# A two-layer decoder trunk on one core: the masked link of the triangular inversion is made on ScalarE before the row chain, not on GpSimd within it

## The chip, the cores and the metric

The kernel runs on one core of one Trainium2 chip. The metric is device time in microseconds (us) of one execution; lower is better. The kernel before takes 1342.59 us (median of 3 runs, 1339.93 to 1345.52). All times below are us unless marked ns.

## What is computed

A decoder trunk with two layers on 256 tokens of width 1024, batch 1, all in float32. Each layer applies three sub-layers, each followed by a residual layer norm:

```
x <- LN(alpha*x + 0.5*SwiGLU_1(x))      # width 2816
x <- LN(alpha*x + Mixer(x))
x <- LN(alpha*x + 0.5*SwiGLU_2(x))
```

The mixer projects its input with one wide matrix and sums three gated branches: an RWKV-7 recurrence (8 heads of 64), a chunked gMLP and an RG-LRU recurrence. The recurrence of RWKV-7 is what matters here:

```
def step(state, inp):
    sa = einsum('bhvk,bhk->bhv', state, -kk_t)
    state = state * w_t + sa (x) (kk_t * a_t) + v_t (x) k_t
    return state, einsum('bhvk,bhk->bhv', state, r_t)
```

## The kernel before, in words

**Matrix products.** Each float32 product is made from three products of split halves: a weight block of 128 x 1024 is loaded by SyncE's DMA queue (`raw`, 3 buffers), ScalarE casts its high half (`whi`, L91), VectorE subtracts to get the low half (`wlo`, L93), and TensorE multiplies (L205 to L207). The blocks come in the fixed order of their use and are converted some blocks ahead.

**The mixer as a chain and a filler.** `Mixer.run` advances two generators. The chain (`rwkv`) is the recurrence: it is turned into chunks of 64 tokens, and for each chunk and head a unit lower-triangular 64 x 64 matrix must be inverted (`invert`), 32 of them in all, after which four rounds of `step` carry the state on. The filler (`others`) is the rest of the mixer: projections `z`, gates `g`, branch products `p` and the parts of gMLP and RG-LRU (`lx`, `lg`, `ls`, `ly`, `sp`, `ot`). Each `yield` gives an amount of time; the filler is advanced until it has covered it. Chain instructions have a higher priority. A list scheduler then fixes the order of every engine's queue from priorities and its own estimate of times, so a small edit can move instructions of other parts too. On the chip each engine runs its queue strictly in that order.

**The inversion.** It works on blocks of 16 rows. VectorE transposes the scores of each matrix into `X` (L848) and picks the diagonal blocks into `U` (L851, L852; `U` and the growing inverse `Ti` are the two halves of the tile `UT`). Then GpSimd runs the **row chain**: for each of 15 steps a product (L864, `X<-UT`) and a subtraction (L865, `UT<-UT,X`), each waiting for the one before it. VectorE spreads the result to a 32-row layout (L882, `X<-UT`) and transposes it twice (L885 into `Rd`, L886 into `Tt`). TensorE multiplies `UB` by `Tt` (L892, tile `y`), ScalarE copies it (L894, `Y`), TensorE multiplies by `Rd` (L899, `z`), VectorE subtracts (L900) and transposes (L901); a second pair of products (L910, `y`; L917, `z`) makes the 64-row inverse `R`, from which L926 and L938 make what the rounds (`up` L969, `s` L953) read.

`UB` is the **masked link**: the 16 columns 16 to 31 of each 32-column block of scores, with rows 0 to 15 of each 32 set to zero, and zeros in columns 0 to 15. Before, GpSimd makes it in four multiplications by the constant `bmask` (L879), one for each quarter of the partitions, written in the program after the row chain's loop:

```
            for u, h, rows in halves:
                c0 = ca[u] + 32 * h
                pool.tensor_tensor(UB[rows], SC[u][rows, :, c0:c0 + 32],
                                   T.bmask[rows].rearrange("p (a b) -> p a b", a=1).to_broadcast([32, 16, 32]), ALU.mult)
```

The scheduler places them within the row chain on GpSimd's queue.

Of the kernel before, what the change touches and what calls it, by code (L numbers as in the profile page):

```python
# [9 lines left out]
AF = mybir.ActivationFunctionType  # L10
ALU = mybir.AluOpType
PSUM = bass.MemoryType.PSUM
P = 128
# [102 lines left out]
class Trunk:  # L116
# [33 lines left out]
    def mixer_constants(self):  # L150
        nc, const = self.nc, self.const

        def t(name, shape):
            return const.tile(shape, F32, name=name)

        pool = nc.gpsimd
        self.identr = const.tile([P, P], F32R, name="identr")
        nc.vector.tensor_copy(self.identr, self.ident)

        self.ones64 = t("ones64", [P, P])  # L160
        self.mean64 = t("mean64", [P, P])
        for tl, v in ((self.ones64, 1.0), (self.mean64, 1.0 / 64)):
            pool.memset(tl, 0.0)
            for h in range(2):
                pool.memset(tl[64 * h:64 * h + 64, 64 * h:64 * h + 64], v)


        rar = t("smask", [P, 3, 64])
        pool.memset(rar, 1.0)
        for rows in (slice(0, 64), slice(64, P)):  # L170
            pool.affine_select(out=rar[rows], in_=rar[rows], compare_op=ALU.is_ge, fill=0.0, base=0,
                               pattern=[[0, 3], [1, 64]], channel_multiplier=-1)
            pool.affine_select(out=rar[rows, 1, :], in_=rar[rows, 1, :], compare_op=ALU.is_ge, fill=0.0, base=-1,
                               pattern=[[1, 64]], channel_multiplier=-1)
        self.smask = [rar[:, u:u + 2].rearrange("p a b -> p (a b)") for u in range(2)]

        self.restart = t("restart", [P, 8, C])
        pool.memset(self.restart, 1.0)
        pool.memset(self.restart[:, :, 0:1], 0.0)

        self.bsel = t("bsel", [P, 2])
        pool.memset(self.bsel, 0.0)
        for h in range(4):

            pool.affine_select(out=self.bsel[32 * h:32 * h + 32, 0:1], in_=self.bsel[32 * h:32 * h + 32, 0:1],
                               compare_op=ALU.is_ge, fill=1.0, base=-16, pattern=[[0, 1]], channel_multiplier=1)
            pool.affine_select(out=self.bsel[32 * h:32 * h + 32, 1:2], in_=self.bsel[32 * h:32 * h + 32, 1:2],
                               compare_op=ALU.is_ge, fill=1.0, base=15, pattern=[[0, 1]], channel_multiplier=-1)

        self.bmask = t("bmask", [P, 32])  # L190
        pool.memset(self.bmask, 0.0)
        nc.vector.tensor_scalar(self.bmask[:, 16:32], self.bmask[:, 16:32], self.bsel[:, 0:1], None, ALU.add)

        self.hsel = t("hsel", [P, 2])
        pool.memset(self.hsel, 0.0)
        for h in range(4):
            pool.memset(self.hsel[32 * h:32 * h + 32, h % 2:h % 2 + 1], 1.0)
# [325 lines left out]
class Mixer:  # L523
# [156 lines left out]
    def rwkv(self):  # L680
        T, nc, l = self.T, self.nc, self.l
        v, act, mmul = nc.vector, nc.scalar, nc.tensor.matmul
        zwa, k, r, vv = self.zwa, self.k, self.r, self.v
        w2, a2 = self.w2a2[0:64], self.w2a2[64:P]
        sg, a, n2, ARV, BK, PC, bonus, Ps, Pis = {}, {}, {}, {}, {}, {}, {}, {}, {}
# [108 lines left out]
        SC, BKT, AT, SV, W1, W2T, O = {}, {}, {}, {}, {}, {}, {}  # L794
# [45 lines left out]
        def invert():  # L840

            pool = nc.gpsimd
            units, halves = [slice(0, 64), slice(64, P)], [(u, h, slice(64 * u + 32 * h, 64 * u + 32 * h + 32)) for u in range(2) for h in range(2)]
            ca = [64, 0]
            X = self.mt([P, 16, 32], "X")
            for u, h, rows in halves:
                c0 = ca[u] + 32 * h
# [3 lines left out]
            v.tensor_scalar_mul(U, X[:, :, 0:16], T.bsel[:, 0:1])  # L851
            v.scalar_tensor_tensor(U, X[:, :, 16:32], T.bsel[:, 1:2], U, ALU.mult, ALU.add)  # L852

            pool.memset(Ti, 0.0)
            pool.affine_select(out=Ti, in_=Ti, compare_op=ALU.not_equal, fill=1.0, base=0, pattern=[[1, 16], [-1, 16]],
                               channel_multiplier=0)
# [4 lines left out]
            for t in range(15):  # L861
# [11 lines left out]
                    act.copy(xx[q], px)  # L873
                if t % 2:
                    yield 1.4
            UB = self.mt([P, 16, 32], "UB")
            for u, h, rows in halves:
                c0 = ca[u] + 32 * h
                pool.tensor_tensor(UB[rows], SC[u][rows, :, c0:c0 + 32],  # L879
                                   T.bmask[rows].rearrange("p (a b) -> p a b", a=1).to_broadcast([32, 16, 32]), ALU.mult)  # L880
            for b in range(2):
                v.tensor_scalar_mul(E[:, :, 16 * b:16 * b + 16], Ti, T.bsel[:, b:b + 1])  # L882
            R = self.sp.tile([P, 16, 64], F32, tag="b4", name=T.n("R"), bufs=2)
# [6 lines left out]
            for n in range(16):  # L890
                for u, h, rows in halves:
                    mmul(ps[rows, n, :], UB[rows, n, :], Tt[rows, n, :], start=True, stop=True)  # L892
            Y = self.mt([P, 16, 32], "Y")
# [150 lines left out]
        yield from scaled(tune["prep"], scores(1))  # L1044
        bonus_of(1)
        yield from scaled(tune["inv"], invert())
        yield from scaled(tune["step"], both(chunks(0), chunks(1)))
        yield from scaled(tune["post"], both(post(0), post(1)))
# [375 lines left out]
```

## Time and profile before

| | value |
|---|---|
| median of 3 runs | 1342.59 us (1339.93 to 1345.52) |
| the profiled execution's own time | 1344.46 us |
| its span in the trace | 1342.7 us |
| mean granted TensorE clock | 0.986 |
| TensorE busy | 1304.1 us (97%) |
| VectorE busy | 847.1 us (63%) |
| ScalarE busy | 647.6 us (48%) |
| GpSimd busy | 96.6 us (7%) |
| mean busy share of the 16 DMA engines, HBM traffic | 56%, 170 GB/s |

The profiled execution took 1344.46 us; the 1.8 us beside its span lie outside the recorded instructions. Busy time is the time in which an engine had an instruction under way. "Granted clock" is the share of TensorE's full clock of 2.4 GHz that the chip gave it; 0.5 is its lower level, 1.2 GHz. An average over the whole span hides the two mixers, which run from about 240 to 460 us and from about 890 to 1120 us; the rows below come mostly from them.

### The profile page before, as it was taken

The page shows a single profiled execution, that of the slowest core. Times are in us where ns is not written, and L with a number is a line of the kernel's source. Part 1 is how long each engine was busy: PE and PEld are TensorE (multiplying, and loading weights), DVE is VectorE, ACT ScalarE, POOL GpSimd, SP SyncE. Part 2 cuts the span into 40 slices and gives each one's busy share as a digit, 9 for nine tenths or more (in the row PEclk, how much of TensorE's full clock was granted, in tenths as well). Part 3 has the DMA queues.
Part 4 walks back from the last instruction along what each step waited for, and adds up shares of the span by engine and source line. Part 5 has one row for each costly group of instructions (what it writes and reads, how often), then busy time and mean ns, then how long its engine had stood idle before and what let it go on. Part 6 is the DMA issues. An engine that isn't in the chain of part 4 may idle for free.

```text
span 1342.7 us, 25628 instructions
## 1 busy us (share of the span) xinstructions
PE 1304.1 (97%) x10807; PEld 1231.3 (92%) x10807; DVE 847.1 (63%) x1144; ACT 647.6 (48%) x865; POOL 96.6 (7%) x154
## 2 busy tenths in 40 slices
PE   8999999997899999999999999999969999999997
PEld 8999999996899999999899999999968998999996
DVE  5655576777576665454665555777866667664444
ACT  5545436643844545344445354375448454444441
POOL 1000000005000020000000000001050002100000
PEclk9999999989999999999999999999979999999999
DMA  7686654634236647766646776464432466477661
GB/s 242 207 255 202 207 168 133 182 95 126 65 111 193 209 147 220 220 188 186 192 138 208 243 213 203 125 186 129 126 95 65 146 200 208 140 230 218 191 188 52
DMA packets 184548, 229.98 MB, mean 171 GB/s; under 512 B 8144, under 2 KB 165840, under 8 KB 184432
## 3 DMA queue, kind: packets, MB, share of 16 engines
q1 hardware_dynamic: 183792, 226.24, 55.2%
q0 software_dynamic: 640, 2.10, 0.6%
q8 instruction: 85, 1.39, 0.4%
q14 instruction: 31, 0.25, 0.1%
HBM read 227.26 MB, written 1.05 MB: 170 GB/s over the span
## 4 chain that ended last, share of the span: by engine, by line
PE 87%; ACT 4%; DVE 3%; POOL 3%; DMA 2%; issue 1%; SPq 0%; DVEq 0%; ACTq 0%; POOLq 0%
PE w L206 11%; PE w L205 11%; PE w L207 11%; PE dn L207 6%; PE dn L206 6%; PE dn L205 6%; PE gate L206 3%; PE gate L207 3%; PE gate L205 3%; PE zr L207 2%; PE zr L206 2%; PE zr L205 2%; DMA raw<-in_ffn_w_dram 2%; PE pb L205 2%; PE pb L207 2%; PE pb L206 2%
## 5 line engine op out<-in xcount | busy, mean ns | idle before, releaser
L93 DVE TENSOR_TENSOR wlo<-raw,whi 128x1024 fp32r<-128x1024 f32 (+1 forms) x314 | 381.9, 1220 | 241.0 <-ACT whi L91 239.1
L91 ACT CAST whi<-raw 128x1024 fp32r<-128x1024 f32 (+1 forms) x322 | 331.5, 1033 | 361.3 <-DMA raw<-in_ffn_w_dram 131.8
L205 PE MATMUL w<-xT,whi 128*128 128x256 f32 x1280 | 363.1, 284 | 0.0
L206 PE MATMUL w<-xT,whi 128*128 128x256 f32 x1280 | 362.8, 283 | 0.0
L207 PE MATMUL w<-xT,wlo 128*128 128x256 f32 x1280 | 362.8, 283 | 0.0
L206 PEld LDWEIGHTS w<-xT,whi 128*128 128x128 f32 x1280 | 245.9, 192 | 1.5
L205 PEld LDWEIGHTS w<-xT,whi 128*128 128x128 f32 x1280 | 246.0, 192 | 1.2
L207 PEld LDWEIGHTS w<-xT,wlo 128*128 128x128 f32 x1280 | 246.1, 192 | 0.0
L93 DVE TENSOR_TENSOR w<-raw,w 128x1024 fp32r<-128x1024 f32 x88 | 107.7, 1224 | 124.3 <-ACT w L91 123.8
L91 ACT CAST w<-raw 128x1024 fp32r<-128x1024 f32 x88 | 92.3, 1048 | 134.5 <-DMA raw<-in_ffn_w_dram 131.8
L205 PE MATMUL dn<-w,g 128*128 128x512 f32 x352 | 137.4, 390 | 0.4 <-ACT g L210 0.4
L206 PE MATMUL dn<-w,g 128*128 128x512 f32 x352 | 137.4, 390 | 0.0
L207 PE MATMUL dn<-w,g 128*128 128x512 f32 x352 | 136.6, 391 | 0.0
L205 PE MATMUL gate<-xT,whi 128*128 128x256 f32 x384 | 111.2, 290 | 1.8 <-DVE xc L1138 1.8
L207 PE MATMUL gate<-xT,wlo 128*128 128x256 f32 x384 | 111.3, 290 | 0.0
L206 PE MATMUL gate<-xT,whi 128*128 128x256 f32 x384 | 111.1, 289 | 0.0
L207 PEld LDWEIGHTS dn<-w,g 128*128 128x128 f32 x352 | 66.1, 188 | 14.1 <-DVE g L211 0.3
L205 PEld LDWEIGHTS dn<-w,g 128*128 128x128 f32 x352 | 66.3, 188 | 13.2 <-ACT g L210 1.0
L205 PEld LDWEIGHTS gate<-xT,whi 128*128 128x128 f32 x384 | 75.0, 195 | 2.9 <-issue 2.8
L206 PEld LDWEIGHTS dn<-w,g 128*128 128x128 f32 x352 | 66.1, 188 | 12.3
L206 PEld LDWEIGHTS gate<-xT,whi 128*128 128x128 f32 x384 | 74.8, 195 | 0.9 <-issue 0.2
L207 PEld LDWEIGHTS gate<-xT,wlo 128*128 128x128 f32 x384 | 74.9, 195 | 0.7 <-issue 0.2
(335 smaller groups left out, 2281.0 us busy)
## 6 DMA issues: line engine op xcount, KB each, us to landing
raw<-in_ffn_w_dram SPq DMA_DIRECT2D x264, 512.0 KB, 4.5
raw<-in_w_in_dram SPq DMA_DIRECT2D x108, 512.0 KB, 4.2
raw<-in_p_branch_dram SPq DMA_DIRECT2D x24, 512.0 KB, 3.8
raw<-in_w_out_dram SPq DMA_DIRECT2D x16, 512.0 KB, 4.3
ln_g<-in_ln_g_dram SPq DMA_DIRECT2D x8, 256.0 KB, 5.2
ln_b<-in_ln_b_dram SPq DMA_DIRECT2D x8, 256.0 KB, 6.1
bd<-in_bd_dram SPq DMA_DIRECT2D x6, 256.0 KB, 5.4
ln_g<-in_ln_g_dram POOLq DMA_DIRECT2D x4, 256.0 KB, 4.3
```

The source lines that it names most:

```text
L91: self.last_act = self.nc.scalar.copy(hi[:, s:s + w], t[:, s:s + w]).ins
L93: eng.tensor_tensor(lo[:, s:s + w], t[:, s:s + w], hi[:, s:s + w], ALU.subtract)
L205: mm(out, a[0], b[0], start=start, stop=False)
L206: mm(out, a[0], b[1], start=False, stop=False)
L207: mm(out, a[1], b[0], start=False, stop=stop)
```

## The change

`UB` is made by ScalarE, ahead of the row chain. GpSimd sets its columns 0 to 15 to zero, and ScalarE copies columns 16 to 31 with a scale per partition (`bsel`, 1 or 0), one ACTIVATE with the function Identity for each quarter of the partitions. The four multiplications and the constant `bmask`, with its memset on GpSimd and its fill on VectorE, are gone. `UB` is allocated before `xx`, so the tiles of the mixer's pool that follow it lie in other slots.

```
@@ mixer_constants
-        self.bmask = t("bmask", [P, 32])
-        pool.memset(self.bmask, 0.0)
-        nc.vector.tensor_scalar(self.bmask[:, 16:32], self.bmask[:, 16:32], self.bsel[:, 0:1], None, ALU.add)
@@ invert
             v.scalar_tensor_tensor(U, X[:, :, 16:32], T.bsel[:, 1:2], U, ALU.mult, ALU.add)
 
+            UB = self.mt([P, 16, 32], "UB")
+            pool.memset(UB[:, :, 0:16], 0.0)
+            for u, h, rows in halves:
+                c0 = ca[u] + 32 * h
+                act.activation(UB[rows, :, 16:32], SC[u][rows, :, c0 + 16:c0 + 32], AF.Identity, scale=T.bsel[rows, 0:1])
+
             pool.memset(Ti, 0.0)
...
                 if t % 2:
                     yield 1.4
-            UB = self.mt([P, 16, 32], "UB")
-            for u, h, rows in halves:
-                c0 = ca[u] + 32 * h
-                pool.tensor_tensor(UB[rows], SC[u][rows, :, c0:c0 + 32],
-                                   T.bmask[rows].rearrange("p (a b) -> p a b", a=1).to_broadcast([32, 16, 32]), ALU.mult)
```

The change also moves instructions in the scheduler's order. Outside the stretch from the inversion to the end of each mixer's rounds the queues hold the same instructions in the same order, save for the dropped constant. Line numbers after the edits differ by 3 or 4 (L882 is L879 after, L899 is L896).

VectorE's queue in the first mixer, at the end of the row chain, before (`X<-UT` is the first instruction behind the row chain, `wlo` a low half of a weight, `xc` a step of the RG-LRU convolution, `ogT` gMLP's output):

```order
L93 TENSOR_TENSOR wlo_3676<-raw_3582,whi_3675 128x1024
L1138 SCALAR_TENSOR_TENSOR xc_3574<-lx_3575,vecs_1159,xc_3574 128x255
L93 TENSOR_TENSOR wlo_3960<-raw_3667,whi_3959 128x1024
L1138 SCALAR_TENSOR_TENSOR xc_3574<-lx_3575,vecs_1159,xc_3574 128x254
L1138 SCALAR_TENSOR_TENSOR xc_3574<-lx_3575,vecs_1159,xc_3574 128x253
L882 TENSOR_SCALAR X_3416<-UT_3421,bsel 128x16x16 x2
L885 STREAM_TRANSPOSE Rd_3741<-X_3416 128x16x2x16
L886 STREAM_TRANSPOSE Tt_3742<-Rd_3741 128x512
L1123 SCALAR_TENSOR_TENSOR ogT_3007<-ogt_3747,ogT_3005 128x2x128
```

and the same place now:

```order
L879 TENSOR_SCALAR X_3413<-UT_3418,bsel 128x16x16 x2
L882 STREAM_TRANSPOSE Rd_3739<-X_3413 128x16x2x16
L93 TENSOR_TENSOR wlo_3679<-raw_3585,whi_3678 128x1024
L1135 SCALAR_TENSOR_TENSOR xc_3577<-lx_3578,vecs_1156,xc_3577 128x255
L883 STREAM_TRANSPOSE Tt_3740<-Rd_3739 128x512
L93 TENSOR_TENSOR wlo_3958<-raw_3670,whi_3957 128x1024
L1135 SCALAR_TENSOR_TENSOR xc_3577<-lx_3578,vecs_1156,xc_3577 128x254
L1120 SCALAR_TENSOR_TENSOR ogT_3004<-ogt_3745,ogT_3002 128x2x128
L1135 SCALAR_TENSOR_TENSOR xc_3577<-lx_3578,vecs_1156,xc_3577 128x253
```

The two weight halves and the three `xc`, which stood ahead of the row chain's end, now stand behind it; one `wlo` and one `xc` come between `Rd` and `Tt`.

VectorE's queue in the second mixer, at the same point, before (`u` is a gMLP product):

```order
L1111 SCALAR_TENSOR_TENSOR u_10859<-sg_11015,vecs_8478,u_10859 128x128 x4
L93 TENSOR_TENSOR wlo_11105<-raw_10847,whi_11104 128x1024
L93 TENSOR_TENSOR wlo_11111<-raw_10853,whi_11110 128x1024
L882 TENSOR_SCALAR X_10629<-UT_10634,bsel 128x16x16 x2
L93 TENSOR_TENSOR wlo_11476<-raw_11102,whi_11475 128x1024
L885 STREAM_TRANSPOSE Rd_10996<-X_10629 128x16x2x16
L886 STREAM_TRANSPOSE Tt_10997<-Rd_10996 128x512
```

and now:

```order
L1108 SCALAR_TENSOR_TENSOR u_10863<-sg_11014,vecs_8476,u_10863 128x128 x3
L879 TENSOR_SCALAR X_10627<-UT_10632,bsel 128x16x16 x2
L1108 SCALAR_TENSOR_TENSOR u_10863<-sg_11014,vecs_8476,u_10863 128x128
L93 TENSOR_TENSOR wlo_11104<-raw_10851,whi_11103 128x1024
L882 STREAM_TRANSPOSE Rd_10995<-X_10627 128x16x2x16
L883 STREAM_TRANSPOSE Tt_10996<-Rd_10995 128x512
```

Here one `wlo` stays between `X` and `Rd`, the fourth `u` joins it, and two weight halves move behind `Tt`.

TensorE's queue in the first mixer around the product `z`, before (`gate` and `ly` are filler):

```order
L205 MATMUL gate_3956<-xT_160_2136,whi_3584 128x256
L206 MATMUL gate_3956<-xT_161_2137,whi_3584 128x256
L899 MATMUL z_3850<-Rd_3741,Y_3848 32x32 x64
L207 MATMUL gate_3956<-xT_160_2136,wlo_3585 128x256
L205 MATMUL gate_3956<-xT_160_2136,whi_3584 128x256
```

and now:

```order
L202 MATMUL ly_4183<-xT_161_2134,whi_3672 128x256
L203 MATMUL ly_4183<-xT_160_2133,wlo_3673 128x256
L896 MATMUL z_3848<-Rd_3739,Y_3846 32x32 x64
L201 MATMUL ly_4183<-xT_160_2133,whi_3672 128x256
L202 MATMUL ly_4183<-xT_161_2134,whi_3672 128x256
```

`z` stood behind 20 matmuls of the gate; it now stands behind all 48 of the gate and 9 of the next block, 37 filler matmuls later. In the rounds after the inversion the filler between the first `up` and the first `s` shrinks from 23 matmuls to 10. The four ACTIVATEs of `UB` stand on ScalarE's queue in the first mixer behind the cast before the first copy `xx`, in the second ahead of the gate's ACTIVATE before it; both are ahead of the row chain's first step.

## Rows read from the trace of the kernel before

**Rows 1.** The page, part 1: engine, busy time (share of the span), instructions.

```profile
PE 1304.1 (97%) x10807; PEld 1231.3 (92%) x10807; DVE 847.1 (63%) x1144; ACT 647.6 (48%) x865; POOL 96.6 (7%) x154
```

**Rows 2.** Waits of TensorE, whole span: us in total, times, longest.

```profile
PE y L892 <- DVE Tt L886: 14.9, 2, 8.3
PE lg L1144 <- issue: 3.5, 1, 3.5
PE y L910 <- DVE Tt L901: 1.9, 1, 1.9
...
PE gate L205 <- DVE xc L1138: 1.8, 1, 1.8
PE up L969 <- ACT gq L1055: 1.6, 1, 1.6
PE w L926 <- ACT R L919: 1.6, 2, 1.5
```

**Rows 3.** Timeline, GpSimd, first mixer: start, us, engine, line, operation, count.

```profile
320.58 1.27 POOL L879 TENSOR_TENSOR UB<-sc,bmask 32x512 f32<-32x512 f32 x1
...
322.20 5.67 POOL L879 TENSOR_TENSOR UB<-sc,bmask 32x512 f32<-32x512 f32 x3
327.95 0.30 POOL L864 TENSOR_TENSOR X<-UT 128x63 f32<-128x63 f32 x1
...
332.58 0.22 POOL L865 TENSOR_TENSOR UT<-UT,X 128x15 f32<-128x15 f32 x1
```

**Rows 4.** Timeline, VectorE, first mixer; the bracket is idle time ahead, and its releaser.

```profile
322.57 1.99 DVE L93 TENSOR_TENSOR wlo<-raw,whi 128x1024 fp32r<-128x1024 f32 x1 [1.48 <-ACT whi L91]
...
326.68 0.99 DVE L1138 SCALAR_TENSOR_TENSOR xc<-lx,vecs,xc 128x254 f32<-128x254 f32 x2
332.83 0.62 DVE L882 TENSOR_SCALAR X<-UT,bsel 128x256 f32<-128x256 f32 x2 [5.16 <-POOL UT L865]
333.48 1.04 DVE L885 STREAM_TRANSPOSE Rd<-X 128x512 f32<-128x512 f32 x1
334.55 0.71 DVE L886 STREAM_TRANSPOSE Tt<-Rd 128x512 f32<-128x512 f32 x1
```

**Rows 5.** Timeline, GpSimd, second mixer.

```profile
981.88 7.17 POOL L879 TENSOR_TENSOR UB<-sc,bmask 32x512 f32<-32x512 f32 x4
...
995.95 0.22 POOL L865 TENSOR_TENSOR UT<-UT,X 128x15 f32<-128x15 f32 x1
```

**Rows 6.** Timeline, VectorE, second mixer.

```profile
983.32 1.11 DVE L1111 SCALAR_TENSOR_TENSOR u<-sg,vecs,u 128x128 f32<-128x128 f32 x4
...
996.20 0.62 DVE L882 TENSOR_SCALAR X<-UT,bsel 128x256 f32<-128x256 f32 x2 [4.36 <-POOL UT L865]
996.73 1.22 DVE L93 TENSOR_TENSOR wlo<-raw,whi 128x1024 fp32r<-128x1024 f32 x1
...
998.94 0.71 DVE L886 STREAM_TRANSPOSE Tt<-Rd 128x512 f32<-128x512 f32 x1
```

**Rows 7.** Stretches of 5 us: busy us (instructions) of each engine, granted clock, DMA.

```profile
315.00:320.00 5.00, 5.00 (x45) 5.00 (x44) 4.92 (x10) 2.41 (x3) 4.29 (x10) 1.00 0.63 178
```

**Rows 8.** The same for the second mixer.

```profile
985.00:990.00 5.00, 5.00 (x32) 5.00 (x32) 1.56 (x1) 0.47 (x1) 4.61 (x6) 0.70 0.68 231
...
1000.00:1005.00 5.00, 5.00 (x136) 4.12 (x127) 2.89 (x8) 3.29 (x9) 0.00 (x0) 0.50 0.24 84
```

**Rows 9.** Timeline, ScalarE, both mixers.

```profile
306.92 1.05 ACT L91 CAST whi<-raw 128x1024 fp32r<-128x1024 f32 x1 [3.33 <-issue]
...
359.38 1.21 ACT L919 ACTIVATE R<-z 32x512 f32<-32x512 f32 x2
...
972.94 0.58 ACT L873 COPY xx<-x 128x512 f32<-128x512 f32 x1 [4.13 <-PE x L872]
```

**Rows 10.** Timeline, TensorE, second mixer, around the products of the inversion.

```profile
999.80 1.93 PE L892 MATMUL y<-Tt,UB 32*32 32x32 f32 x128 [8.35 <-DVE Tt L886]
...
1008.79 1.20 PE L910 MATMUL y<-Tt,sc 32*32 32x32 f32 x64
```

## The prediction

> **What bounds the kernel now.** I read the engine totals first [rows 1]: TensorE is busy for 1304.1 of the span's 1342.7 us, so almost all of the time is matmuls that the change doesn't touch, and at most 38.6 us can be won by filling holes. The list of TensorE's waits [rows 2] says where the holes are. The largest entry by far is `y` at L892, the first product behind the row chain: 14.9 us in two waits for `Tt`, 8.3 in the second mixer and so 6.6 in the first. The other entries of 1.6 or more name `lg`, the second `y`, a `gate`, `up` and `w`, all in the mixers; none names a weight. The timelines then tell what `Tt` waits for: VectorE stands idle for 5.16 ahead of `X` in the first mixer [rows 4] and for 4.36 in the second [rows 6], each time released by the last subtraction of the row chain on GpSimd. So in these two places, and hardly anywhere else, the row chain sets the end, and everything that stretches it is paid by TensorE, less what filler it still has.
>
> **UB leaves the row chain.** In the first mixer its four multiplications take 1.27 + 5.67 = 6.94 [rows 3]; the instructions overlap at their edges by about 0.1, so the chain's end moves forward by 6.85, from 332.80 (the start 332.58 and its 0.22) to 325.95. In the second they are one block of 7.17 [rows 5], of which 7.13 is delay: the end moves from 996.17 to 989.04. Together 13.98. That is what the row chain wins; what reaches TensorE is less, because the queue behind the row chain changes too.
>
> **Behind the row chain, first mixer.** VectorE's order now reads `X`, `Rd`, a weight half, an `xc`, `Tt`. From 325.95: `X` 0.65 (0.62 and a gap), `Rd` 1.07 [rows 4], the weight half 1.22 as the one in [rows 6], `xc` 0.49 (half of the pair at 326.68), `Tt` 0.71 [rows 4]: 4.14, so `Tt` ends at 330.1. Before it ended at 335.26 (334.55 + 0.71). So 5.2 arrives of 6.85; the inserted pair costs the other 1.7. TensorE's idle time there was 3.5 (`lg`) and 6.6 (`y`), together 10.1 ahead of `y`. The `lg` waited for a PSUM bank that the last `xc` frees; the new order gives it the bank of the gate, so this wait goes, but its time only joins the one before `y`, and 10.1 falls to 4.9. Then the second `y` waited 1.9 [rows 2]; `z` now stands 37 matmuls later, which at 5.00/45 = 0.11 each [rows 7] is 4.1 of cover, and I take 0.15 for it. `up` waited 1.6; with the chain earlier and the filler moved I take 0.5. The three `xc` stand later than before, and a gMLP product, which now takes the bank of `lx`, will wait for the last of them: 0.45 by my walk. Sum: 5.2 + 1.75 + 1.1 - 0.45 = 7.6, less some 0.2 of gaps, **7.4**.
>
> **Behind the row chain, second mixer.** From 989.04: `X` 0.65, one `u` 0.28 (a quarter of 1.11), the weight half 1.22, `Rd` 1.04, `Tt` 0.71 [rows 6]: 3.9, so `Tt` ends at 992.95 against 999.65 (998.94 + 0.71): 6.7 earlier. The wait of 8.35 [rows 10] falls to 1.6; the 1.6 for `R` and the 1.8 of the gate [rows 2] I leave. Of 6.7 I take **6.5**, because the two weight halves put behind `Tt` must still be made.
>
> **The clock.** After the long wait the granted clock is at its lower level: 0.50 for 1000 to 1005 [rows 8], where `y` takes 1.93 [rows 10]. Also behind the gate's wait of 1.8 it is 0.70, with 32 matmuls in 5 us [rows 8] against 45 at full clock [rows 7]: 13 x 0.11 = 1.5 us lost to one dip. Shorter waits may save such dips, later ones may bring new ones. In both rows the fall follows a wait. I take one dip net lost, with the thinner filler below: **-1**.
>
> **What is added, and what hides it.** ScalarE gets four ACTIVATEs in each mixer. No row has this shape; the nearest above is `R`, two of 32x512 in 1.21 [rows 9], 0.60 each for as many elements as the new ones have on twice the columns read, so 0 to 2.4 per mixer. Nothing excludes that all is hidden: in the second mixer they stand ahead of a copy `xx` that ScalarE stood idle for 4.13 before [rows 9]; in the first behind a cast ahead of which it was idle for 3.33 [rows 9], with smaller gaps after. If this cover is gone, weight casts move back by at most 4.8 in both, and TensorE has no weight wait of note to lengthen [rows 2]. I take 0. GpSimd's memset of half of `UB` writes fewer elements per partition than one multiplication of 1.27 [rows 3], and GpSimd is busy for 96.6 of 1342.7 [rows 1]: 0. The constant's memset and fill happen before the first product; 0, at most 0.25 gained. No DMA is added or moved.
>
> In the rounds after the inversion the filler between the first `up` and the first `s` falls from 23 matmuls to 10: 13 x 0.11 = 1.5 of cover gone from each of eight rounds; the waits that bound those rounds don't appear in [rows 2], so most of them keep cover to spare, and what this costs is in the 1 above.
>
> **Sum.** 7.4 + 6.5 - 1 = 13 us. The profiled execution's own time is 1344.46, so it would read 1331.5; it lies 1.9 above the median of the runs, 1342.59, and the forecast as a median is **1329.6**. With the clock at its worst and ScalarE's 4.8 half uncovered it is 1333; with the whole 13.98 and two dips saved, 1326. That is the forecast's own range.
>
> **Rivals.** *Port contention passes on to the chain.* While `UB` runs, weight halves on VectorE are long: 1.99 against 1.22 [rows 4, 6]. The same may happen to the row chain itself: it now meets casts that were met by `UB`. A step of the chain that meets one loses something between 0.5 (a quarter of 7.17, 1.79, against the 1.27 of the first multiplication in [rows 3]) and the 1.22 that a weight half takes [rows 6]; I take 0.9, about the middle. Four such meetings cost 3.6: gain 9.4, time 1333. Against it: the weight halves stand behind `X` now. The Trainium skill (SBUF — State Buffer, section "SBUF: two separate sides") says that VectorE and GpSimd share one port pair as an exclusive lock, held for a whole instruction. By that rule every cast that starts first stops the row chain for its full length, and the trace agrees in that casts and `UB` lengthen each other. Chance 0.12.
>
> *The gain is given back.* TensorE runs ahead of the weights: if it arrives 13 us earlier at a stretch where blocks come just in time, it waits for them instead, and the time is 1338 to 1343. In 985 to 990 the DMA engines are busy for 0.68 and move 231 GB/s [rows 8], above the average of the whole run, so a local shortage is possible. Against it stands that TensorE's list of waits names no weight of note [rows 2]. The Trainium skill (SBUF — State Buffer, section "A bandwidth-pool intuition that's wrong (but worth ruling out)") says HBM is almost always the end-to-end bottleneck; by that rule the transfers would set the end and nothing be won, and the trace disagrees so far as TensorE is busy for 97% with no wait on a block. Chance 0.21.
>
> *Slower: the rounds lose their cover.* If each of the eight rounds now shows its uncovered 1.5 and a dip of the clock like that behind the gate's wait, 1.5 more, they cost 3 each: 8 x 3.06 = 24.5, against 13 won, so +11.5 and 1354. It decides from the fifth round on (13/3.06 = 4.2). For it: the order shows the thinner filler. Against it: no round's wait is in [rows 2] but `up` once, so a round must first use up cover that it has. Chance 0.04.
>
> *The change doesn't do what it says.* `y` needs `UB`; were ScalarE so late that `UB` came after `Tt`, the wait would only change its name and the time stay near 1342. `UB` should be there by 310, 20 us ahead. Chance 0.03.
>
> **How the numbers follow.** About 0.60 for the forecast (1326 to 1333). With 0.12 for the port, of which most lies at 1333, this is 0.72; down to 1325 and up to 1340 the range takes in part of the case of gains given back, and leaves out its upper half, the slower case and the unchanged one. 0.5% is 6.7 us, about what a measurement of this kernel can tell from no change: faster means below 1335.9. Faster: 0.60 and 0.12 and a little of the given-back case, 0.75. Slower 0.04. The rest, 0.21, is the same.
>
> **What would show it.** Right: no `UB` on GpSimd within the row chain, whose fifteen steps run unbroken; TensorE's wait at `y` (L889 after the edits) falls from 14.9 to some 6.5 in all, the longest from 8.3 to 4.9; `Tt` ends at 330 and 993 on the same scale of time; `lg`'s wait of 3.5 is gone; the span falls by about as much as TensorE's idle time. Wrong: `Tt` as early as said but TensorE's idle time about 38 again, with entries for weights (given back) or `s` and `up` (rounds); or the row chain with gaps beside casts (port); or `y` waiting for ScalarE's `UB`. A span that falls with TensorE's busy time, not its idle time, would mean that the clock was mis-sized.

## The result and the profile after

The changed kernel takes 1329.11 us (median of 4 runs, 1328.05 to 1331.55) against 1344.05 before in the same comparison: a ratio of 0.989, with a 95% interval from 0.988 to 0.991. The forecast was 1329.6, the range 1325 to 1340. Two later comparisons gave 0.988 (0.987 to 0.990) and 0.990 (0.988 to 0.992); over all 14 runs the median is 1329.4. In the traces shown, the span fell from 1342.7 to 1326.3, 16.4 us: more than the change itself brings, as the runs below show.

Engine totals of the changed kernel, to be read beside [rows 1]:

```profile
PE 1302.3 (98%) x10807; PEld 1228.9 (93%) x10807; DVE 844.0 (64%) x1143; ACT 650.7 (49%) x873; POOL 83.9 (6%) x147
```

TensorE's idle time, span less busy, fell from 38.6 to 24.0, by 14.6, and its busy time by only 1.8. So time was won mostly by filling holes, and the list of TensorE's waits (us in total, times, longest) says which:

```profile
PE y L889 <- DVE Tt L883: 6.3, 2, 4.0
PE gate L201 <- DVE xc L1135: 1.8, 1, 1.8
...
PE up L966 <- ACT gq L1052: 1.0, 1, 1.0
PE lg L1141 <- PE y L889: 0.9, 1, 0.9
PE y L907 <- DVE Tt L898: 0.8, 1, 0.8
...
PE lg L1141 <- ACT gate L1198: 0.5, 1, 0.5
```

Against [rows 2], `y` fell from 14.9 to 6.3, `lg` from 3.5 to 1.4 (0.5 in the first mixer, and 0.9 in the second, where it did not wait before), the second `y` from 1.9 to 0.8, `up` from 1.6 to 1.0. No weight has come onto the list.

GpSimd in the first mixer (start, us, engine, line, operation), against [rows 3]; L866 and L867 are the row chain's L864 and L865:

```profile
312.22 1.18 POOL L867 TENSOR_TENSOR UT<-UT,X 128x55 f32<-128x55 f32 x1
...
316.03 0.30 POOL L866 TENSOR_TENSOR X<-UT 128x64 f32<-128x64 f32 x1
316.41 0.32 POOL L867 TENSOR_TENSOR UT<-UT,X 128x64 f32<-128x64 f32 x1
316.81 0.31 POOL L866 TENSOR_TENSOR X<-UT 128x63 f32<-128x63 f32 x1
...
321.45 0.22 POOL L867 TENSOR_TENSOR UT<-UT,X 128x15 f32<-128x15 f32 x1
```

Where `UB` stood, between the product 128x64 and the next 128x63, the steps now follow each other every 0.4 us. The row chain takes 13.5 us (308.18 to 321.67) against 20.1; in the second mixer 13.2 against 20.5. Its first step in each mixer, in the kernel before and then in the changed one:

```profile
312.72 0.23 POOL L864 TENSOR_TENSOR X<-UT 128x15 f32<-128x15 f32 x1 [29.87 <-DVE UT L852]
975.67 0.23 POOL L864 TENSOR_TENSOR X<-UT 128x15 f32<-128x15 f32 x1 [36.77 <-DVE UT L852]
```

```profile
308.18 0.23 POOL L866 TENSOR_TENSOR X<-UT 128x15 f32<-128x15 f32 x1 [29.39 <-DVE UT L848]
965.43 0.22 POOL L866 TENSOR_TENSOR X<-UT 128x15 f32<-128x15 f32 x1 [29.53 <-DVE UT L848]
```

One kind of stall stays: three steps in each mixer take about 1.2 instead of 0.3, as the step at 312.22 does. VectorE ran a weight half then, from 311.94 to 313.22. The row chain before had three such steps in each mixer too.

VectorE behind the row chain, first mixer, then second, against [rows 4] and [rows 6]:

```profile
321.70 0.62 DVE L879 TENSOR_SCALAR X<-UT,bsel 128x256 f32<-128x256 f32 x2 [4.89 <-POOL UT L867]
322.36 1.04 DVE L882 STREAM_TRANSPOSE Rd<-X 128x512 f32<-128x512 f32 x1
323.25 1.20 DVE L93 TENSOR_TENSOR wlo<-raw,whi 128x1024 fp32r<-128x1024 f32 x1
324.38 0.46 DVE L1135 SCALAR_TENSOR_TENSOR xc<-lx,vecs,xc 128x255 f32<-128x255 f32 x1
324.76 0.69 DVE L883 STREAM_TRANSPOSE Tt<-Rd 128x512 f32<-128x512 f32 x1
...
978.71 0.62 DVE L879 TENSOR_SCALAR X<-UT,bsel 128x256 f32<-128x256 f32 x2 [4.78 <-POOL UT L867]
979.24 0.35 DVE L1108 SCALAR_TENSOR_TENSOR u<-sg,vecs,u 128x128 f32<-128x128 f32 x1
979.50 1.22 DVE L93 TENSOR_TENSOR wlo<-raw,whi 128x1024 fp32r<-128x1024 f32 x1
980.64 1.05 DVE L882 STREAM_TRANSPOSE Rd<-X 128x512 f32<-128x512 f32 x1
981.72 0.71 DVE L883 STREAM_TRANSPOSE Tt<-Rd 128x512 f32<-128x512 f32 x1
```

`Tt` ends 3.8 us behind the row chain in both mixers; the prediction had 4.1 and 3.9. The two fillings that it named, a weight half with an `xc`, and a `u` with a weight half, stand there.

TensorE at `y`, and ScalarE's four ACTIVATEs of `UB` in each mixer:

```profile
325.59 1.93 PE L889 MATMUL y<-Tt,UB 32*32 32x32 f32 x128 [3.98 <-DVE Tt L883]
...
982.58 1.40 PE L889 MATMUL y<-Tt,UB 32*32 32x32 f32 x128 [2.27 <-DVE Tt L883]
```

```profile
303.58 2.06 ACT L854 ACTIVATE UB<-sc,bsel 32x256 f32<-32x256 f32 x4
...
958.11 2.06 ACT L854 ACTIVATE UB<-sc,bsel 32x256 f32<-32x256 f32 x4
```

An ACTIVATE takes 0.52, and `UB` is there 20 us before `y` wants it.

Not all of the 16.4 us came from there. At its first step the row chain of the changed kernel is already 4.5 us ahead (308.18 against 312.72), and up to some 30 us ahead of it the queues hold the same instructions, but for the constant's two. The stretch before it in the kernel before (us, busy us and instructions of PE, PEld, DVE, ACT, POOL, granted clock, DMA share, GB/s):

```profile
260.00:270.00 10.00, 10.00 (x77) 9.23 (x76) 8.66 (x15) 3.75 (x7) 1.64 (x1) 0.89 0.52 154
270.00:280.00 10.00, 10.00 (x53) 9.55 (x52) 2.75 (x6) 2.08 (x4) 0.00 (x0) 0.60 0.01 2
```

and in the changed kernel:

```profile
260.00:270.00 10.00, 10.00 (x83) 9.20 (x83) 8.88 (x16) 4.04 (x8) 1.63 (x1) 1.00 0.55 155
270.00:280.00 10.00, 10.00 (x83) 9.40 (x82) 6.28 (x12) 5.16 (x8) 1.09 (x4) 1.00 0.10 28
```

TensorE was busy throughout in both, but before it was given its lower level from about 267 to 278 and did 53 matmuls instead of 83 in the second ten us. To keep this apart, the experiments compare two intervals: from the start of the row chain's first step to the start of the last `rs` on GpSimd in the layer norm behind the same mixer. From the kernel before to the changed one these went from 173.2 to 168.0 and from 173.9 to 167.7: 5.1 and 6.2. With the 4.5 ahead and 0.6 between the two mixers that is the 16.4.

### The profile page after: what moved, and what is told of

The parts are those of the page before. It is cut to its first block, busy times and chain, and to the rows that moved or that the text cites. A ratio compares the mean times of both kernels' runs of the same rounds, so it can differ in the third digit from the quotient of the medians.

```text
span 1326.3 us, 25625 instructions
## 1 busy us (share of the span) xinstructions
PE 1302.3 (98%) x10807; PEld 1228.9 (93%) x10807; DVE 844.0 (64%) x1143; ACT 650.7 (49%) x873; POOL 83.9 (6%) x147
## 4 chain that ended last, share of the span: by engine, by line
PE 91%; DVE 3%; ACT 3%; POOL 2%; issue 1%; DMA 0%; SPq 0%; DVEq 0%; ACTq 0%; POOLq 0%
PE w L202 12%; PE w L201 12%; PE w L203 12%; PE dn L203 6%; PE dn L202 6%; PE dn L201 6%; PE gate L202 3%; PE gate L201 3%; PE gate L203 3%; PE zr L203 2%; PE zr L202 2%; PE zr L201 2%; PE pb L201 2%; PE pb L202 2%; PE pb L203 2%
## 5 line engine op out<-in xcount | busy, mean ns | idle before, releaser
L201 PE MATMUL gate<-xT,whi 128*128 128x256 f32 x384 | 110.0, 286 | 1.8 <-DVE xc L1135 1.8
L202 PE MATMUL gate<-xT,whi 128*128 128x256 f32 x384 | 109.5, 285 | 0.0
L201 PEld LDWEIGHTS dn<-w,g 128*128 128x128 f32 x352 | 66.2, 188 | 12.7 <-ACT g L206 0.4
L201 PEld LDWEIGHTS gate<-xT,whi 128*128 128x128 f32 x384 | 73.5, 191 | 3.0 <-issue 2.7
L202 PEld LDWEIGHTS gate<-xT,whi 128*128 128x128 f32 x384 | 73.5, 191 | 0.7 <-issue 0.2
```

The source lines that it names most:

```text
L201: mm(out, a[0], b[0], start=start, stop=False)
L202: mm(out, a[0], b[1], start=False, stop=False)
```

## The experiments

**The theory**: TensorE waits at `y`, so the row chain's length is paid one for one, and `UB` within it was that length; which engine makes `UB` doesn't matter. **Rivals**: the engine (VectorE is relieved of a competitor), the new slots and orders, or the clock.

| kernel | row chain, mixer 1 and 2 | interval, mixer 1 and 2 | median |
|---|---|---|---|
| before | 20.1, 20.5 | 173.2, 173.9 | 1344.1 |
| before again | 20.3, 20.6 | 173.6, 175.4 | 1344.3 |
| changed | 13.5, 13.2 | 168.0, 167.7 | 1329.1 |
| changed again | 13.5, 13.3 | 168.0, 167.7 | 1328.5 |
| changed, third | 13.5, 13.3 | 167.9, 167.7 | 1330.6 |
| slot only | 20.3, 20.6 | 173.6, 174.0 | 1344.3 |
| GpSimd, ahead of the chain | 15.2, 14.4 | 169.0, 170.0 | 1333.5 |
| ScalarE, behind the loop | 13.7, 14.5 | 169.6, 167.4 | 1331.7 |
| five multiplications more | 19.1, 18.3 | 174.3, 173.0 | 1340.4 |
| ten multiplications more | 23.0, 24.3 | 175.3, 179.3 | 1347.7 |
| ACTIVATEs made twice | 13.7, 13.5 | 169.9, 169.8 | 1332.5 |
| less filler between the steps | 13.5, 14.2 | 177.4, 191.9 | 1364.5 |
| last three steps on VectorE | 13.5, 15.4 | 169.5, 174.5 | 1336.6 |
| all steps on VectorE | 16.7, 15.3 | 170.1, 174.9 | 1337.6 |

Row chain and intervals are differences of starts and ends in the timeline of one trace each. The medians come from four comparisons, in which the kernel before had 1344.1 (with "changed"), 1344.2 (with "before again", "changed again", "slot only" and "GpSimd"), 1343.0 (with ScalarE, the multiplications and the ACTIVATEs) and 1342.7 (with the others).

**Both kernels again.** No edit.

> The kernel before, unchanged, to see its spread and whether the fall of the clock at 268 to 278 us of its trace (0.50, with the same order of instructions as in the changed kernel, where it stays at 1.00) comes back. Theory (the change is worth what the row chain wins, about 11.3 us in the two traces outside this fall; the fall is chance): the ratio is 1.000 within 0.002, and a second trace need not show the fall. Rival (the fall belongs to the kernel before and is part of the gain): every trace shows it at the same place.

> The changed kernel, unchanged, for a larger sample. Theory (gain of the row chain alone, 11 to 12 us): ratio 0.991 to 0.992. Rival (the clock is part of the gain): 0.988 to 0.990, as in the first comparison.

> The changed kernel again, to see with more runs whether its profile shows the fall of the clock at 266 to 278 us. Theory (chance, likelier in the kernel before): median 1327 to 1330; a trace with the fall would read some 4.5 us more than one without. Rival (the changed kernel never has it): all runs within 1326 to 1330 and no trace shows it.

The kernel before, again: 1.000 (0.998 to 1.001). Its second trace has the fall of the clock too, 0.95 and 0.71 in the two stretches. The changed kernel gave 0.988 (0.987 to 0.990) and 0.990 (0.988 to 0.992). The first of these lies in the rival's range and outside the theory's, which had counted the row chain alone; its trace has no fall. The third trace of the changed kernel has the fall as well:

```profile
260.00:270.00 10.00, 10.00 (x80) 9.10 (x79) 8.40 (x15) 3.50 (x6) 1.65 (x1) 0.95 0.51 150
270.00:280.00 10.00, 10.00 (x66) 9.78 (x64) 3.83 (x7) 3.45 (x6) 0.00 (x0) 0.71 0.01 2
```

So the fall is no property of the kernel before: the rival that the changed kernel never has it is out. By the start of the row chain it cost this trace some 2 to 2.5 against the other two, not the 4.5 expected; its median, 1330.6, is just above the 1330 that was the upper end. The two traces with the same fall make the fair pair: spans 1342.9 and 1328.9, 14.0 apart. By the intervals of three traces each of the order before (two, and slot only) and of the changed kernel, the mixers gain 5.5 and 6.7, together 12.2. The medians are 14.9, 15.8 and 12.1 apart in the three comparisons. Whether the fall is likelier before isn't settled: three traces of three had it with the order before, one of three with the changed kernel, and three of the eight other variants below.

**Where, or on which engine.** The multiplications stay on GpSimd and move ahead of the loop:

```
+            UB = self.mt([P, 16, 32], "UB")
+            for u, h, rows in halves:
+                c0 = ca[u] + 32 * h
+                pool.tensor_tensor(UB[rows], SC[u][rows, :, c0:c0 + 32],
...
             pool.memset(Ti, 0.0)
```

> The kernel before with its four multiplications still on GpSimd, but written and queued ahead of the row chain. Theory (place): GpSimd idles for 29.9 us ahead of the row chain, so the 5 to 7 us of multiplications are hidden there, the row chain runs unbroken, and the time is that of the changed kernel, ratio 0.989 to 0.993. Rival (engine): what counts is that GpSimd no longer competes with VectorE's weight halves; then the multiplications lengthen VectorE's transposes ahead of the row chain by about as much as they did before, it starts up to 5 us later in each mixer, and the ratio is 0.996 to 1.000.

0.992 (0.991 to 0.993): 10.7 of the 15.8 that the changed kernel gained in the same comparison, and 8.9 of 12.2 by the intervals, with GpSimd doing as much as before. Its multiplications are hidden well ahead of the row chain's start at 312.20:

```profile
282.06 3.20 POOL L857 TENSOR_TENSOR UB<-sc,bmask 32x512 f32<-32x512 f32 x2
300.10 4.69 POOL L857 TENSOR_TENSOR UB<-sc,bmask 32x512 f32<-32x512 f32 x2 [14.85 <-DVE sc L811]
```

The 5 us that it lacks are partly in the row chain itself, 15.2 and 14.4 long: five and four of its steps, not three, meet a weight half, because VectorE's order came out another way. In its trace the clock also fell ahead of the mixer (0.66 in 270 to 280). So the place carries two thirds of the gain or more. How much of the rest is the engine isn't parted here from the order and the clock.

**The slots alone.** Only the allocation line moves, as in the diff above, and the multiplications stay behind the loop.

> The kernel before with one line moved: the tile UB is allocated ahead of xx, as in the changed kernel, and the four multiplications stay where they are, on GpSimd within the row chain. Theory: the slots of the tiles carry none of the gain; ratio 0.997 to 1.003, TensorE's waits at y 14 to 16 us in all. Rival (the tiles' new slots and the order that follows from them bring part of the gain): ratio under 0.996.

1.000 (0.999 to 1.001). The tiles' slots carry nothing.

**ScalarE, but written behind the loop.** The allocation, the memset and the ACTIVATEs stand where the multiplications stood.

```
-            UB = self.mt([P, 16, 32], "UB")
-            pool.memset(UB[:, :, 0:16], 0.0)
...
                 if t % 2:
                     yield 1.4
+            UB = self.mt([P, 16, 32], "UB")
+            pool.memset(UB[:, :, 0:16], 0.0)
```

> The changed kernel with the four ACTIVATEs and the allocation of UB written behind the row chain's loop, where the multiplications stood before. Theory (what counts is that nothing stands within the row chain on GpSimd): ratio 0.989 to 0.993, like the changed kernel. Rival (they must be ahead of the row chain, else y waits for ScalarE): y waits for UB instead of Tt, ratio 0.995 to 1.000.

0.991 (0.988 to 0.993), as the theory had it. ScalarE's queue has the ACTIVATEs within the row chain's time (from 315.6 and 975.5), and `y` waits for `Tt`, 6.0 us in all, never for `UB`. So either half of the change, the engine or the place, would have freed the row chain.

**The row chain made longer again.** In the changed kernel, inside the loop:

```
+                if t == 7:
+                    for _ in range(5):
+                        pool.tensor_tensor(E[:, :, 16:32], U, Ti, ALU.mult)
```

> The changed kernel with five multiplications of 128x256 put into the row chain after its eighth step, each of which must wait for the step before; their results go to a half of X that nothing reads before it is overwritten. At an estimated 0.7 to 0.8 us each (from 1.27 for 32x512 and 0.32 for 128x63) the row chain grows by about 3.7 us. Theory (TensorE waits at y, so the row chain's length is paid there, up to what the order behind it gives): the time grows by 4 to 7.5 us over the changed kernel, ratio 0.992 to 0.996. Rival (the gain came from the order and the clock, not from the row chain): 0.988 to 0.991.

> The same with ten such multiplications, about 7.4 us, which is what UB took within the row chain before. Theory: the time of the kernel before comes back, ratio 0.997 to 1.003, and the difference to the changed kernel is about twice that of five. Rival: 0.988 to 0.993.

Five: 0.998 (0.997 to 0.999); ten: 1.003 (1.001 to 1.004). GpSimd in the first mixer with five, and with ten:

```profile
316.76 0.75 POOL L878 TENSOR_TENSOR X<-UT 128x256 f32<-128x256 f32 x1
...
317.73 4.88 POOL L878 TENSOR_TENSOR X<-UT 128x256 f32<-128x256 f32 x4
```

```profile
320.48 0.73 POOL L878 TENSOR_TENSOR X<-UT 128x256 f32<-128x256 f32 x1
...
321.44 8.89 POOL L878 TENSOR_TENSOR X<-UT 128x256 f32<-128x256 f32 x9
```

Alone one takes 0.75, as estimated; where weight halves run beside it, about 1.0 to 1.2. So the row chain grew by more than was expected. Five missed the expected ratio upwards; ten came out within it, at its edge; and the times are 11 and 18 us above the changed kernel's, not one twice the other. The theory holds better than its numbers: against the changed kernel the two row chains together are 10.6 and 20.6 longer, the two intervals together 11.6 and 18.9. The order before lies near, with 13.8 and 11.3 in its first trace, and 14.1 with 13.3 and 11.9 in the two others. So here 0.8 to 1.1 us of time come with each us of row chain. The last four rows of the table lie off this line: there the edits moved other work too, as told below.

**The ACTIVATEs made twice.**

```
+            for u, h, rows in halves:
+                c0 = ca[u] + 32 * h
+                act.activation(UB[rows, :, 16:32], SC[u][rows, :, c0 + 16:c0 + 32], AF.Identity, scale=T.bsel[rows, 0:1])
```

> The changed kernel with the four ACTIVATEs of UB made twice. Theory (they are hidden on ScalarE; the prediction's cost of 0): the same as the changed kernel, ratio 0.989 to 0.992. Rival (uncovered, the prediction's bound of 2.4 us per mixer, here once more): 4.8 us more, ratio 0.993 to 0.996.

0.992 (0.990 to 0.994), some 3 to 4 us more, at the upper edge of the theory's range. But the order moved too: in the second mixer three `u` now stand behind `X`, so the filler itself waits for the row chain.

```profile
981.47 0.58 PE L201 MATMUL gate<-xT,whi 128*128 128x256 f32 x1 [8.48 <-DVE u L1111]
```

That wait takes the place of the one at `y`. In the first mixer `up` waits 3.4 for ScalarE's `gq` instead of 1.0. What the second set of ACTIVATEs costs by itself stays open; the prediction's 0 for the first set rests on the changed kernel's trace alone.

**Towards a faster version.** Three tries shorten what stands ahead of `y`: less filler between steps (`yield 1.4` to `yield 1.0`), the last three steps on VectorE (`(pool if t < 12 else v)` in both lines of the loop), and all of them (`t < 0`).

> The changed kernel with the filler between the steps of the row chain cut from 1.4 to 1.0; by the order X, Rd and Tt then stand together on VectorE in the second mixer and only one weight half stands between them in the first. Theory (the path to y is row chain plus what stands between X and Tt): Tt comes 0.5 us earlier in the first mixer and 1.5 in the second, so up to 2 us less than the changed kernel where the filler still lasts, ratio 0.986 to 0.990. Rival (filler is what is short: 47 matmuls fewer stand ahead of y in the second mixer, 47 x 0.12 = 5.6 us): TensorE waits longer at y and the time grows by 2 to 5 us, ratio 0.990 to 0.993.

> The changed kernel with the last three of the row chain's fifteen steps on VectorE instead of GpSimd. Theory (the row chain's length is paid one for one, and VectorE stands idle for 4.8 us ahead of X): the row chain ends up to 1.5 us earlier per mixer, but two weight halves slip in between X and Tt in the first mixer, 1.2 us more than now; together 0 to 2 us less, ratio 0.987 to 0.990. Rival (VectorE's queue holds the steps up behind weight halves that wait for ScalarE): 2 us or more longer, ratio 0.990 to 0.994.

> The changed kernel with all fifteen steps on VectorE. No step can then meet a weight half at the shared port, but each must queue behind those that the order puts between the steps: five weight halves and nine xc, 10.6 us, beside thirty steps of an estimated 0.2, together 16.6 against 13.5 on GpSimd in the first mixer. Theory: 1 to 4 us longer than the changed kernel, ratio 0.989 to 0.993. Rival (the meetings at the port are what makes the chain slow, three per mixer of 0.95): 2 to 5 us shorter, ratio 0.985 to 0.988.

None beats the changed kernel. The last three on VectorE: 0.996 (0.994 to 0.997), worse than even the rival said. A step's instruction takes 0.2 there, but the row chain gets no shorter: 13.5 in the first mixer as on GpSimd, and 15.4 in the second, where three weight halves, an `xc` and four `u` are queued among its last six instructions:

```profile
975.93 0.20 DVE L866 TENSOR_TENSOR X<-UT 128x39 f32<-128x39 f32 x1 [4.66 <-POOL UT L867]
...
981.51 0.17 DVE L867 TENSOR_TENSOR UT<-UT,X 128x15 f32<-128x15 f32 x1
```

A product of the filler waits there too. The trace names a step of the row chain as what ended the wait; a `gate` doesn't read that, so it may have been the `xc` queued just ahead of the step:

```profile
977.81 0.55 PE L201 MATMUL gate<-xT,whi 128*128 128x256 f32 x1 [5.40 <-DVE UT L867]
```

All on VectorE: 0.996 (0.995 to 0.998), worse than expected. The row chain takes 16.7 in the first mixer (306.71 to 323.37), as worked out, and in the second `X` is followed by a weight half that waits 2.74 for ScalarE:

```profile
981.55 0.62 DVE L879 TENSOR_SCALAR X<-UT,bsel 128x256 f32<-128x256 f32 x2
984.91 1.22 DVE L93 TENSOR_TENSOR wlo<-raw,whi 128x1024 fp32r<-128x1024 f32 x1 [2.74 <-ACT whi L91]
986.05 1.04 DVE L882 STREAM_TRANSPOSE Rd<-X 128x512 f32<-128x512 f32 x1
```

So in these rows the three meetings with weight halves cost less than a queue shared with them. Less filler gave 1.017 (1.015 to 1.019), far beyond either expectation: `y` waits 14.2 us again, and TensorE's busy time, 1322.8, is 20.5 longer. The last section shows most of why.

## Why the prediction was right

**What bounds the kernel** was read rightly: `y` behind the row chain. The stalls put back show it from the other side.

**UB leaves the row chain.** Forecast 6.85 and 7.13, measured 6.6 and 7.3 as the change of its length, 13.8 against 13.98 together.

**Behind the row chain.** From the first step to the end of `Tt` the first mixer took 22.54 (312.72 to 335.26) and takes 17.27: 5.3 won, 5.2 forecast. The second took 23.98 and takes 17.00: 7.0 won, 6.7 forecast. The waits at `y` were to be 4.9 and 1.6 and are 4.0 and 2.3. `lg`'s wait of 3.5 did not go whole: 0.5 is left, now for ScalarE's `gate`, and a new wait of 0.9 stands behind `y` in the second mixer. The second `y` still waits 0.8, not 0.15, and `up` 1.0, not 0.5: the cover that `z` got was priced too high. The wait for `R` that I left at 1.6 fell to 0.5, and a gMLP product waits 0.2 for the last `xc`.

**The mixers' sums.** Second: 6.5 forecast, 6.2 in the first pair of traces, 6.7 over three each. First: 7.4 forecast, 5.1 and 5.5: this is the term that was mis-sized. TensorE's idle time in 316 to 376 did fall by 6.8 (13.9 to 7.1, summed over stretches of 2 us), but not all of it became time. In this pair of traces the clock has a part in that: its low stretch moved. Before, it lay mostly over the wait:

```profile
330.00:335.00 5.00, 0.00 (x0) 0.00 (x0) 2.10 (x4) 0.00 (x0) 2.17 (x9) 0.50 0.03 9
335.00:340.00 5.00, 4.59 (x138) 4.24 (x139) 2.12 (x5) 3.62 (x10) 0.00 (x0) 0.55 0.02 3
```

Now TensorE works in it:

```profile
325.00:330.00 5.00, 4.21 (x136) 3.84 (x137) 3.60 (x8) 2.69 (x9) 0.00 (x0) 0.50 0.74 204
330.00:335.00 5.00, 5.00 (x33) 4.62 (x32) 3.00 (x6) 3.76 (x9) 0.00 (x0) 0.84 0.03 10
```

TensorE worked 4.1 us at the lower level in the first interval before and 5.8 now; at half the speed the difference is worth 0.9 of the 1.7 lost. But the two other traces of the order before have 7.4 there and show no smaller gain, so the clock is not the whole answer. Over both intervals and three traces each, idle time fell by 13.7 on the mean (27.5 to 13.8), where the forecast without its 1 for the clock had 13.9: the holes were sized rightly in sum. Busy time in the intervals rose by 1.5 (320.4 to 321.9), and that is what the gain lacks. It is not the dip that I took as lost: work at the lower level was 12.7, 15.0 and 12.3 before and 11.8, 11.7 and 11.7 now. So the 1 us was about the right size for a wrong reason, and what makes up the 1.5 stays open. The sum of the two mixers is 12.2 measured and 13 forecast.

**The hit is closer than the working.** That the median came out within 0.5 of the forecast is luck. The forecast started from 1342.59, and in the comparison itself the kernel before had 1344.05; and the median changed by 14.9 there (15.8 and 12.1 later), 2.7 above what the mixers gain. In the profiled pair part of that is the clock's fall ahead of the first mixer, which the profiled execution before had and I did not look for: 4.5 us of its own 16.4.

**ScalarE, the memset, the constant, the slots** cost nothing that a trace of the changed kernel shows. **The rounds** kept their cover: none appears in the list of waits but `up`. (13 x 0.11 is 1.4, not 1.5, so the rival of the rounds would have cost about 23, not 24.5; nothing hangs on it.)

**The rivals.** *Port contention passes on*: no more meetings than before, three in each row chain, so nothing was passed on here; but the mechanism is real, and in the kernel with GpSimd ahead of the chain its two meetings more lengthened a row chain by 1.7. The Trainium skill (SBUF — State Buffer, section "SBUF: two separate sides") says that when VectorE's instruction has two SBUF inputs, as a weight half has, whichever of the two engines starts first holds the shared ports for its whole instruction while the other blocks; the trace agrees, since the step at 312.22 ends at 313.40, just behind the weight half that ended at 313.22. The three `xc` from 310.51 to 312.02, which read one input from PSUM, the memory that TensorE writes, lengthened none of the four steps beside them (0.27 to 0.30). *Given back*: from the end of the first mixer to the next row chain the changed kernel gains 0.6 more, and behind the second nothing is lost: no weight is waited for. That HBM is nearly always the bottleneck, which the same page of the Trainium skill says in its section "A bandwidth-pool intuition that's wrong (but worth ruling out)", is not borne out in this kernel, at 56% of the DMA engines' time. *Slower* and *doesn't do what it says* are out by the rows above.

## What to carry to other kernels

A chain of small dependent instructions that another engine waits for should hold nothing else: what it needs later can be queued ahead of it, on the same engine or on an idle one, and most of its length then comes back (here 12.2 us of 14.0, by three traces each). Read what the scheduler will queue between the chain's end and its consumer, since some of the gain is lost there. And before a difference of two traces is put down to a change, look at the stretches that the change can't reach.

## What was not expected of the hardware

**The clock fell under a busy TensorE.** From about 268 on it was at its lower level for some 7 to 10 us in some traces and not in others of the same order, with no idle time before it; what TensorE did just before were the scores and small 128x2 products. It cost 2 to 4.5 us by the start of the row chain.

**Alternating two kinds of matmul is dear.** With less filler ahead, the rounds' products were queued singly among filler ones. TensorE in the second mixer of that kernel:

```profile
1042.97 0.28 PE L203 MATMUL gate<-xT,wlo 128*128 128x256 f32 x1
1043.09 0.28 PE L201 MATMUL gate<-xT,whi 128*128 128x256 f32 x1
...
1045.06 0.38 PE L201 MATMUL pb<-ogT,whi 128*128 128x256 f32 x1
1045.37 0.33 PE L950 MATMUL s<-state,w2t 64*64 64x64 f32 x2
1045.62 0.39 PE L202 MATMUL pb<-ogT,whi 128*128 128x256 f32 x1
1045.94 0.32 PE L954 MATMUL o<-arv,state 64*64 64x64 f32 x2
```

At full clock a filler matmul starts every 0.12 after another, but 0.31 passes from a filler one to a 64x64 pair and 0.25 back. Not all of the 20.5 us is this: TensorE worked 22.2 us at its lower level there against 11.8 in the changed kernel (summed from the traces), which at half the speed is an estimated 5 of them. The Trainium skill (TensorEngine Tiling (Array Packing), section "Key Properties") says that a change of tiling mode drains TensorE; the rows fit that. No run here parts the drain from the change of data type.
